# One 256-column matmul in place of two 128-column ones in the state and direct-output products of an S5 layer, with the second partial sum added by VectorE

## The chip, the cores and the metric

The kernel runs on one core of one Trainium2 chip. The metric is the device time of one execution in microseconds (us). Before the change it is 2616.41 us, the median of three runs (2616.41 to 2618.24). In the text TensorE is PE, with PEld for its weight loads, VectorE is DVE, ScalarE is ACT, GpSimd is POOL and SyncE is SP, which issues nearly all DMAs. Each engine works through its own queue strictly in the order in which the program wrote it; engines wait for each other by semaphores.

## The reference

An attention block, a gated linear attention block and an S5 block follow one another on a sequence of 1024 tokens and 1024 channels, in float32. The change lies in the S5 block, whose core is

```
u, z   = split(h @ w_in)                       # 2048 channels each, 128 groups of 16
bu     = u32 . b_bar                           # per group: 16 inputs -> 64 complex states
states = associative_scan(a_l*a_r, a_r*b_l + b_r)
y      = Re(states) . c_re - Im(states) . c_im + d * u32
y      = gelu(y);  y = y * sigmoid(y @ w_glu + b_glu) * silu(z);  out = y @ w_out
```

The kernel computes it in chunks of 8 tokens: 128 chunks, one "step" of the recurrence each. For a group, what a chunk adds to its 128 state numbers (64 real, 64 imaginary) is a product of the chunk's 8 x 16 inputs with a 128x128 matrix W. What a chunk's inputs give directly to its own 8 x 16 outputs is a product with a 128x128 matrix T. What the state at the chunk's start gives to the outputs comes later, from a third matrix V.

## The kernel before

Float32 precision on PE comes from splitting each operand into a rounded high part and a low part: `hi` is a cast by ACT (L179), `lo` the difference by POOL (L187, in some stages DVE). A product then takes three matmuls (`mm3`, L194 to L196): high by high, high by low, low by high, all summed in one place of PSUM.

Groups are worked in octets of 8, so there are 16 octets. The first phase of the S5 block (some 1576 to 1860 us in the trace) is a loop of 19 rounds over `first`. In round i the projection generator `project(i)` makes the inputs u of octet i in two halves of 24 matmuls of 512 columns, evacuates each half by ACT (L2165), and writes them to a DRAM scratch (eight DMAs, L2174). From round 3 on the generator `states(i - 3)` works on the octet three rounds back. The two generators are stepped in turn, so PE sees four stretches in one round, called a pass here:

1. the state product U by W of the octet, 8 groups, 24 matmuls of 128 columns into a PSUM tile `big` of 1024 columns; ACT copies it into the state table X (L2214);
2. the first half of the projection;
3. the direct product U by T, again 24 matmuls of 128 columns; ACT copies it into a staging tile `w` (L2222), and SP writes it to the scratch `syp_d` (L2225);
4. the second half of the projection.

There are two `big` tiles in PSUM, so a product can start when the one two places back has been read out.

U, W, T and the projection's weights come through `WStream`: three raw buffers filled by DMA (`wraw`, L100), a ring of six split pieces (`whl`). `pump(n)` issues further loads and splits up to n pieces in the order of use, as far as the ring has room; `release` makes room. Where the calls to `pump` stand in the program sets where the casts stand in ACT's queue and the subtractions in POOL's. Before, `states` calls `pump(2)` right behind the direct product, ahead of the projection's second half.

Beside this, DVE runs the recurrence over the 128 chunks, for four octets at a time (`scan(k)`, L2238 to L2280). One scan is 29 steps: three empty ones (the first issues a DMA for the table `scL`), 15 turns of five instructions over 256 columns, four steps with seven small turns, which read the table `scLP` in SBUF, and seven fix-up steps. A scan is appended after its fourth octet. `scan_on` puts one step behind each of the first two stretches of a pass and two steps behind each of the other two, so six in a pass, as long as there is a scan to run. From octet 4 on the sixteen passes therefore hold two whole scans and the first eleven turns of the third. In the second phase (z projection and the third product) the same goes on with four steps in a round.

The names that the prediction uses: `pairs`, `add_now` and the new `states` of the changed kernel, `scan_on`, `pump`, and the lines above.

Of the kernel before, what the change touches and what calls it, by code (L numbers as in the profile page):

```python
# [16 lines left out]
OP = mybir.AluOpType  # L17
# [6 lines left out]
P = 128  # L24
# [1352 lines left out]
def pool_of(g, stack, name, bufs=1, side="left"):  # L1377
    return stack.enter_context(g.tc.tile_pool(name=name, bufs=bufs, side=side, reuse_waits="tile"))
# [756 lines left out]
def s5(g, xn3, xstack, out):  # L2135
    nc, A, ws = g.nc, g.A, g.ws
# [5 lines left out]
    u_d, spilled, octet, put_m, put_cols, first = (  # L2142
        q.u_d, q.spilled, q.octet, q.put_m, q.put_cols, q.first)
# [14 lines left out]
    def project(i, ids):  # L2158

        W = ws.take(ids)  # L2160
        stage = stg.tile([P, S], F, name="w4")
        for half in range(2):
            ps = g.bank()
            gemm_tr(g, hT, half, W, 0, P, ps, ids if half else None, True, later)
            nc.scalar.activation(half_of(stage, half, True), ps.rearrange("p (t c) -> p t c", t=8),  # L2165
                                 AF.Copy)
            ws.pump(1)
            if half == 0:
                yield
        if i >= NO:  # L2170
            nc.sync.dma_start(z_d[i - NO], stage)
            return
        for j in range(8):
            nc.sync.dma_start(u_d[:, :, i * 8 + j, :].rearrange("t i c -> i t c"),  # L2174
                              stage[j * 16:j * 16 + 16, :].rearrange("p (t c) -> p t c", t=8))
        spilled[i] = True
# [11 lines left out]
    X = pool_of(g, xp, "s5x").tile([P, P, P], F, name="X")  # L2188
# [15 lines left out]
    for half in range(2):  # L2204
        pglu[half] += [put_cols(w_glu, 16, e * P) for e in range(len(pglu[half]), NO)]
        pout.append([ws.put(1, S, [((slice(None),) * 3, g.kview(w_out, k * P, 1, 0, S))]) for k in range(16)])

    def states(o, ids):

        U, W = ws.take(ids[:2])  # L2210
        ps = g.big().rearrange("p (g n) -> p g n", g=8)
        for j in range(8):
            g.mm3(ps[:, j], [a[:, j, :] for a in W], [a[:, j, :] for a in U], True, True)
        nc.scalar.copy(X[:, 1:P, octet(o)], ps.rearrange("p g n -> p n g")[:, 0:P - 1])  # L2214
        del ps
        yield
        T = ws.take(ids)[2]
        yp = stg.tile([P, S], F, name="w4")
        ps = g.big().rearrange("p (g n) -> p g n", g=8)
        for j in range(8):  # L2220
            g.mm3(ps[:, j], [a[:, j, :] for a in U], [a[:, j, :] for a in T], True, True)
        nc.scalar.copy(yp.rearrange("c (g x) -> c g x", g=8), ps)  # L2222
        del ps
        ws.release(ids)
        nc.sync.dma_start(yp_d[o], yp)  # L2225
        ws.pump(2)

# [57 lines left out]
    def scan_on(n):  # L2285

        while n and scans:
            k, ge = scans[0]
            if next(ge, 0) == 0:
                scans.popleft()  # L2290
                scanned[k] = True
            else:
                n -= 1

    for i, px, pp in first:
        gens = [states(i - LAG, px)] if px else []
        gens.append(project(i, pp) if i else begun)
        for r in range(2):
            for ge in gens:
                next(ge, None)  # L2300
                scan_on(1 + r)
        if px and (i - LAG) % 4 == 3:
            scans.append(((i - LAG) // 4, scan((i - LAG) // 4)))

# [16 lines left out]
    def outputs():  # L2321

        o, ps = sums.popleft()
        Xo = X[:, :, octet(o)]
        gto = lambda a: a.rearrange("p (g t o) -> p g t o", g=8, t=8)
        nc.vector.tensor_tensor(Xo.rearrange("p (g o) t -> p g t o", g=8), gto(parts.pop(o)), gto(ps), OP.add)  # L2326
        del ps
        yield
        nc.scalar.activation(Xo, Xo, AF.Gelu_apprx_tanh)

    ws.hi_eng, ws.lo_eng = ["act"], ["pool"]
    for n, (i, ids) in enumerate(second):
        ge, ou = project(NO + i, ids), outputs() if sums else iter(())
# [16 lines left out]
    yp = ExitStack()  # L2350
# [135 lines left out]
    for half in range(2):  # L2486
        hs = slice(half * 512, half * 512 + 512)
        for e in range(NO):
            k0 = glu_k[0] if half == 0 and e == 0 else 0
            ps = accs.pop(e) if k0 else g.bank()  # L2490
# [25 lines left out]
        for k in range(12):  # L2516
            W = ws.take(pout[half][k:k + 1])[0]
# [10 lines left out]
        W = ws.take(pout[half][12:])  # L2528
# [25 lines left out]
def model_kernel(tc, A):  # L2554
    with ExitStack() as ctx:
        g = G(tc, A, ctx)
        g.x2_d = g.dram.tile([S, D], F, name="x2_d")
        g.x3_d = g.dram.tile([S, D], F, name="x3_d")
        with tc.manual_schedule():
            s5_tables(g)  # L2560
            xs = ExitStack()
            xn2 = block1(g, xs)
            xacc, outs = gla(g, xn2, xs, lambda side: s5_prep(g, side))
            s5(g, xacc, outs, A["out"])
# [40 lines left out]
```

## Time and profile before

| | |
|---|---|
| median of three runs | 2616.41 us |
| the profiled execution: its time, its span | 2615.66 us, 2613.9 us |
| busy in the span: PE, PEld, DVE, ACT, POOL | 92%, 76%, 65%, 42%, 43% |
| granted PE clock, mean over the span | 0.964 |
| first octet's state product starts | 1597.37 us |
| last direct product copied by ACT (L2222) | 1853.82 us |

The span is the stretch from the first to the last instruction of the trace; the execution's own time is 1.8 us more. Busy shares are means over stages with different limits, so the stage of the change is read by itself. A matmul's duration in the trace is its latency; matmuls follow each other faster than that, and what one costs is the distance between starts. "[3.10 <-DVE mm]" behind a row says that the engine stood idle for 3.10 us before it and what ended the wait.

### The profile page before, as it was taken

To read this page: it belongs to the slowest core of one execution; us is meant where nothing else is said; L and a number is where in the kernel's file an instruction comes from. 1 tells how busy PE (TensorE), PEld (TensorE's weight loads), DVE (VectorE), ACT (ScalarE), POOL (GpSimd) and SP (SyncE) were. 2 spreads that over 40 slices of the span, in tenths; PEclk is the share of its full clock that TensorE was granted. 3 is DMA by queue.
4 is the path that set the end of the run, shared out by engine and by line. 5 is a ranking of instruction groups with operands and counts; after the bars stand their busy time and mean duration, and the time that the engine had idled before them with its cause. 6 is when DMAs were issued, how large, how long until landed. Compare 5 with 4: busy or idle time off the path is not lost.

```text
span 2613.9 us, 33041 instructions
## 1 busy us (share of the span) xinstructions
PE 2417.1 (92%) x11817; PEld 1990.4 (76%) x11817; DVE 1708.2 (65%) x3015; ACT 1109.5 (42%) x1812; POOL 1127.5 (43%) x826
## 2 busy tenths in 40 slices
PE   5787977999999999999989899999999899999998
PEld 4665755777777777777777678888888788888887
DVE  5889887777454556785777770389788555425642
ACT  5455683656532122324443443444443533323331
POOL 3517465322211566664444424555554433333431
PEclk8998988999999999999989899999999899999999
DMA  8302124221332645535432316777554644444441
GB/s 263 113 30 62 54 87 154 85 65 56 107 122 84 159 136 152 165 122 177 153 113 85 93 69 164 194 202 201 183 154 146 192 133 121 149 139 146 140 149 57
DMA packets 330173, 338.25 MB, mean 129 GB/s; under 512 B 67366, under 2 KB 248182, under 8 KB 329752
## 3 DMA queue, kind: packets, MB, share of 16 engines
q1 hardware_dynamic: 330008, 336.13, 42.2%
q8 instruction: 93, 1.52, 0.2%
q14 instruction: 72, 0.59, 0.1%
HBM read 239.19 MB, written 96.87 MB: 129 GB/s over the span
## 4 chain that ended last, share of the span: by engine, by line
PE 30%; DVE 10%; issue 5%; DMA 3%; POOL 3%; ACT 2%; SPq 0%; POOLq 0%; DVEq 0%; ACTq 0%
PE mm L194 8%; PE mm L196 8%; PE mm L195 8%; PE big L196 2%; PE big L195 2%; PE big L194 2%; POOL whl L187 2%; DMA w<-syp_d 2%; DVE xacc L1998 1%; DVE X L2326 1%; DVE rs_t L215 1%; DVE mm L2257 1%; POOL rs_h L212 1%; DVE mm L2255 1%; DVE rs_t L216 1%
## 5 line engine op out<-in xcount | busy, mean ns | idle before, releaser
L187 POOL TENSOR_TENSOR whl<-wraw,whl 128x1024 fp32r<-128x1024 f32 x183 | 443.3, 2431 | 606.0 <-ACT whl L179 527.3
L179 ACT CAST whl<-wraw 128x1024 fp32r<-128x1024 f32 (+1 forms) x279 | 288.5, 1048 | 360.9 <-PE mm L196 220.0
L194 PE MATMUL mm<-h_hi,whl 128*128 128x512 f32 x768 | 308.0, 401 | 14.5 <-DVE gT L952 7.8
L196 PE MATMUL mm<-h_hi,whl 128*128 128x512 f32 x768 | 302.0, 393 | 0.0
L195 PE MATMUL mm<-h_lo,whl 128*128 128x512 f32 x768 | 301.4, 392 | 0.0
L194 PE MATMUL mm<-whl,h_hi 128*128 128x512 f32 (+1 forms) x720 | 288.4, 400 | 13.0 <-ACT whl L179 9.6
L195 PE MATMUL mm<-whl,h_hi 128*128 128x512 f32 (+1 forms) x720 | 282.1, 392 | 10.8 <-DVE whl L187 10.8
L196 PE MATMUL mm<-whl,h_lo 128*128 128x512 f32 (+1 forms) x720 | 281.1, 390 | 0.0
L187 DVE TENSOR_TENSOR whl<-wraw,whl 128x1024 fp32r<-128x1024 f32 (+2 forms) x96 | 133.4, 1399 | 147.2 <-ACT whl L179 147.1
L194 PE MATMUL mm<-y_hl,whl 128*128 128x512 f32 x512 | 201.3, 393 | 0.0
L195 PE MATMUL mm<-y_hl,whl 128*128 128x512 f32 x512 | 199.9, 390 | 0.0
L196 PE MATMUL mm<-y_hl,whl 128*128 128x512 f32 x512 | 199.8, 390 | 0.0
L194 PEld LDWEIGHTS mm<-h_hi,whl 128*128 128x128 f32 x768 | 146.0, 190 | 49.5 <-DVE gT L952 8.7
L196 PEld LDWEIGHTS mm<-h_hi,whl 128*128 128x128 f32 x768 | 145.5, 189 | 32.2
L195 PEld LDWEIGHTS mm<-h_lo,whl 128*128 128x128 f32 x768 | 146.1, 190 | 29.4 <-issue 0.5
L194 PEld LDWEIGHTS mm<-whl,h_hi 128*128 128x128 f32 x720 | 137.7, 191 | 40.4 <-ACT whl L179 10.1
L195 PEld LDWEIGHTS mm<-whl,h_hi 128*128 128x128 f32 x720 | 138.0, 192 | 36.9 <-DVE whl L187 12.2
L196 PEld LDWEIGHTS mm<-whl,h_lo 128*128 128x128 f32 x720 | 137.3, 191 | 28.5
L187 POOL TENSOR_TENSOR w<-w 128x512 f32<-128x512 f32 x32 | 55.1, 1722 | 168.2 <-ACT w L2434 168.2
L196 PEld LDWEIGHTS mm<-y_hl,whl 128*128 128x128 f32 x512 | 96.5, 189 | 20.1
L194 PEld LDWEIGHTS mm<-y_hl,whl 128*128 128x128 f32 x512 | 97.0, 189 | 19.4
L195 PEld LDWEIGHTS mm<-y_hl,whl 128*128 128x128 f32 x512 | 96.6, 189 | 19.5
(542 smaller groups left out, 5928.8 us busy)
## 6 DMA issues: line engine op xcount, KB each, us to landing
wraw<-in_s_w_glu_dram SPq DMA_DIRECT2D x64, 512.0 KB, 3.9
wraw<-in_gla_w_in_dram SPq DMA_DIRECT2D x40, 512.0 KB, 4.3
wraw<-in_s_w_in_dram SPq DMA_DIRECT2D x32, 512.0 KB, 5.6
wraw<-in_s_w_out_dram SPq DMA_DIRECT2D x32, 512.0 KB, 3.6
gv_d<-stg SPq DMA_DIRECT2D x32, 256.0 KB, 2.2
v_mat<-vc SPq DMA_DIRECT2D x32, 256.0 KB, 2.6
w_mat<-wo SPq DMA_DIRECT2D x32, 256.0 KB, 2.5
gz_d<-stg SPq DMA_DIRECT2D x32, 256.0 KB, 2.1
```

Source lines behind the costliest of these rows:

```text
L179: nc.scalar.copy(out, in_)
L187: e.tensor_tensor(out, a, b, op)
L194: nc.tensor.matmul(out, lhsT=lhs[0], rhs=rhs[0], start=start, stop=False)
L195: nc.tensor.matmul(out, lhsT=lhs[0], rhs=rhs[1], start=False, stop=False)
L196: nc.tensor.matmul(out, lhsT=lhs[1], rhs=rhs[0], start=False, stop=stop)
L212: nc.gpsimd.tensor_tensor(h, v, self.mhalf[:, :n], OP.pow)
L215: nc.vector.tensor_tensor(t, h, h, OP.mult)
L216: nc.vector.tensor_tensor(t, t, v, OP.mult)
L1998: nc.vector.scalar_tensor_tensor(xs, ps[nh], rst, xs, op0=OP.mult, op1=OP.add)
L2255: nc.vector.tensor_tensor(a, x, wide(L[0], n), OP.mult)
L2257: nc.vector.tensor_tensor(c[half[q]], x[half[1 - q]], wide(L[1][half[1 - q]], n), OP.mult)
L2326: nc.vector.tensor_tensor(Xo.rearrange("p (g o) t -> p g t o", g=8), gto(parts.pop(o)), gto(ps), OP.add)
```

## The change

Both products take `mm2` (in the kernel before, but not used by it) in place of `mm3`. Of a split piece, high and low lie side by side in one tile. For each group `mm2` issues one matmul of 256 columns, which multiplies the high part of the fixed operand by the high and the low part of the moving one, into two neighbouring 128-column places of PSUM; a second matmul of 128 columns adds low by high to the second place. A product so leaves two sums. `pairs` works an octet in two halves of four groups, each half in a `big` tile of its own. ACT copies the first sums to their destination (X or the staging tile), and DVE adds the second sums to that destination in place. These additions are not written at once: they are kept in a list, and `add_now` writes them at the next step of `states`. For the state product that is at the head of the direct product, for the direct product it is in a third step at the end of the round, and with it the DMA to `syp_d` and `pump(2)` move there, behind the projection's second half.

```
+    def add_now():
+        for out, ps in adds:
+            nc.vector.tensor_tensor(out, out, ps, OP.add)
+        adds.clear()
+    def pairs(o, lhs, ids, out):
+        for half in range(2):
+            ps = g.big().rearrange("p (j a n) -> p j a n", j=4, a=2)
+            for j in range(4):
+                k = half * 4 + j
+                g.mm2(ps[:, j], [a[:, k, :] for a in lhs], ws.pairs[ids][:, :, k, :])
+            for i in range(2):
+                dst, src = out(half, ps[:, :, i])
+                if i:
+                    adds.append((dst, src))
+                else:
+                    nc.scalar.copy(dst, src)
...
     def states(o, ids):
         U, W = ws.take(ids[:2])
-        ps = g.big().rearrange("p (g n) -> p g n", g=8)
-        for j in range(8):
-            g.mm3(ps[:, j], [a[:, j, :] for a in W], [a[:, j, :] for a in U], True, True)
-        nc.scalar.copy(X[:, 1:P, octet(o)], ps.rearrange("p g n -> p n g")[:, 0:P - 1])
...
+        add_now()
+        pairs(o, W, ids[0], lambda half, ps: (X[:, 1:P, o * 8 + half * 4:o * 8 + half * 4 + 4],
+                                              ps.rearrange("p g n -> p n g")[:, 0:P - 1]))
+        yield
+        ws.take(ids)
         yp = stg.tile([P, S], F, name="w4")
-        ps = g.big().rearrange("p (g n) -> p g n", g=8)
-        for j in range(8):
-            g.mm3(ps[:, j], [a[:, j, :] for a in U], [a[:, j, :] for a in T], True, True)
-        nc.scalar.copy(yp.rearrange("c (g x) -> c g x", g=8), ps)
...
+        add_now()
+        pairs(o, U, ids[2], lambda half, ps: (yp[:, half * 512:half * 512 + 512].rearrange("c (g x) -> c g x", g=4), ps))
         ws.release(ids)
+        yield
+        add_now()
         nc.sync.dma_start(yp_d[o], yp)
         ws.pump(2)
...
+        for ge in gens:
+            next(ge, None)
```

The last two lines stand at the end of a round in the loop over `first`; they run the third step.

The instructions move on two engines. On DVE, at the end of octet 6, where the first scan's turns end and its small turns begin, the queue before is the scan alone:

```order
L2255 TENSOR_TENSOR mm<-X,mm 128x256
L2257 TENSOR_TENSOR mm<-X,mm 64x256 x2
L2258 TENSOR_TENSOR X<-X,mm 128x8x32
L2259 TENSOR_TENSOR X<-X,mm 128x8x32
L2255 TENSOR_TENSOR mm<-X,scLP 128x32
L2257 TENSOR_TENSOR mm<-X,scLP 64x32 x2
L2258 TENSOR_TENSOR X<-X,mm 128x32
L2259 TENSOR_TENSOR X<-X,mm 128x32
```

At the same place of the changed kernel (its scan's lines are 20 higher) the additions of octet 6's direct product (`w`, from the two `big` tiles) stand between the turns:

```order
L2275 TENSOR_TENSOR mm<-X,mm 128x256
L2277 TENSOR_TENSOR mm<-X,mm 64x256 x2
L2278 TENSOR_TENSOR X<-X,mm 128x8x32
L2279 TENSOR_TENSOR X<-X,mm 128x8x32
L2213 TENSOR_TENSOR w_14906<-w_14906,big_14909 128x512
L2213 TENSOR_TENSOR w_14906<-w_14906,big_14919 128x512
L2275 TENSOR_TENSOR mm<-X,scLP 128x32
L2277 TENSOR_TENSOR mm<-X,scLP 64x32 x2
L2278 TENSOR_TENSOR X<-X,mm 128x32
L2279 TENSOR_TENSOR X<-X,mm 128x32
```

Two additions of a product, which no scan step needs, now stand in the scan's queue; four of them come in a pass. On ACT, in the pass of octet 1, the queue before is as follows; `whl_14219` is the weight piece of the next round's projection, and the second L2165 is the evacuation of this round's second half:

```order
L2214 COPY X_13785<-big1024_14133 128x127x8
L2165 ACTIVATE w4_14159<-mm_14160 128x8x64
L2222 COPY w4_14188<-big1024_14189 128x1024
L179 CAST whl_14216<-wraw_14107 128x1024
L179 CAST whl_14219<-wraw_14120 128x1024
L179 CAST whl_14258<-wraw_14186 128x1024
L2165 ACTIVATE w4_14159<-mm_14222 128x8x64
L179 CAST whl_14264<-wraw_14247 128x1024
```

In the changed kernel the same pass reads as follows, and the weight piece of the next projection is `whl_14228`:

```order
L2229 COPY X_13785<-big1024_14123 128x127x4
L2229 COPY X_13785<-big1024_14133 128x127x4
L2165 ACTIVATE w4_14143<-mm_14144 128x8x64
L2229 COPY w4_14174<-big1024_14177 128x512
L2229 COPY w4_14174<-big1024_14187 128x512
L179 CAST whl_14222<-wraw_14108 128x1024
L2165 ACTIVATE w4_14143<-mm_14197 128x8x64
L179 CAST whl_14228<-wraw_14170 128x1024
L179 CAST whl_14251<-wraw_14172 128x1024
L179 CAST whl_14254<-wraw_14226 128x1024
```

The cast of the next projection's weights has moved from ahead of the second half's evacuation to behind it. POOL's subtractions follow the casts in the same order.

## Rows read from the trace of the kernel before

**Rows 1.** Windows: stretch, length, busy and count of each engine, clock, DMA share, GB/s.

```profile
1600.00:1620.00 20.00, 20.00 (x114) 17.37 (x114) 0.00 (x0) 9.51 (x12) 11.89 (x5) 1.00 0.78 200
1680.00:1700.00 20.00, 20.00 (x122) 17.69 (x122) 18.52 (x44) 9.44 (x11) 12.53 (x6) 1.00 0.75 209
```

**Rows 2.** Timeline of PE, octet 0: start, duration, engine, line, operation, wait before.

```profile
1597.37 0.22 PE L194 MATMUL big<-whl 128*128 128x128 f32 x1
...
1599.88 0.28 PE L196 MATMUL big<-whl 128*128 128x128 f32 x1
1600.00 0.45 PE L194 MATMUL mm<-h_hi,whl 128*128 128x512 f32 x1
...
1605.55 0.22 PE L194 MATMUL big<-whl 128*128 128x128 f32 x1
```

**Rows 3.** Timeline of PE, 256-column matmuls of the attention.

```profile
474.30 0.28 PE L1234 MATMUL mm<-pth,v_hl 128*128 128x256 f32 x1
...
474.54 0.28 PE L1234 MATMUL mm<-pth,v_hl 128*128 128x256 f32 x1
```

**Rows 4.** Timeline of DVE, the first scan and the start of the second.

```profile
1675.92 0.23 DVE L2249 COPY mm<-scL 128x64 f32<-128x64 f32 x1 [104.11 <-ACT whl L179]
...
1678.58 0.43 DVE L2255 TENSOR_TENSOR mm<-X,mm 128x256 f32<-128x256 f32 x1
...
1710.80 0.28 DVE L2255 TENSOR_TENSOR mm<-X,scLP 128x32 f32<-128x32 f32 x1
1711.12 2.54 DVE L2257 TENSOR_TENSOR mm<-X,scLP 64x32 f32<-64x32 f32 x2
...
1717.65 0.43 DVE L2257 TENSOR_TENSOR mm<-X,scLP 64x32 f32<-64x32 f32 x2
...
1725.26 0.20 DVE L2273 COPY mm<-X 128x32 f32<-128x32 f32 x1
...
1726.84 0.65 DVE L2280 TENSOR_TENSOR X<-X,mm 128x480 f32<-128x480 f32 x1
1727.53 0.20 DVE L2278 TENSOR_TENSOR mm<-scL,mm 128x32 f32<-128x32 f32 x1
...
1728.99 0.18 DVE L2273 COPY mm<-X 128x32 f32<-128x32 f32 x1
...
1756.88 0.23 DVE L2249 COPY mm<-scL 128x64 f32<-128x64 f32 x1 [5.50 <-DMA scL<-scan_d]
```

**Rows 5.** Groups by form on DVE: shapes, count, busy us, mean ns, idle before.

```profile
L2326 DVE TENSOR_TENSOR X<-w,big 128x1024 f32<-128x1024 f32 x16 | 32.0, 1998 | 17.8 <-DMA w<-syp_d 17.8
...
L298 DVE SCALAR_TENSOR_TENSOR h_lo<-mm,cols,h_hi 128x512 fp32r<-128x512 f32 x32 | 23.2, 748 | 8.2 <-ACT h_hi L297 7.7
...
L952 DVE SCALAR_TENSOR_TENSOR gT<-mm,cols,gT 128x512 f32<-128x512 f32 x8 | 5.7, 743 | 2.1 <-PE mm L951 2.0
```

**Rows 6.** Groups by form, 1600 to 1860 us, on POOL and ACT.

```profile
L187 POOL TENSOR_TENSOR whl<-wraw,whl 128x1024 fp32r<-128x1024 f32 x63 | 149.9, 2396 | 103.5 <-ACT whl L179 93.6 <-DMA wraw<-in_s_w_in_dram 5.7 <-DMA su_d<-w 4.1
...
L179 ACT CAST whl<-wraw 128x1024 fp32r<-128x1024 f32 x64 | 65.5, 1050 | 79.9 <-DMA wraw<-su_d 47.3 <-DMA wraw<-w_mat 23.6 <-POOL whl L187 7.0
...
L2165 ACT ACTIVATE w<-mm 128x512 f32<-128x512 f32 x33 | 19.6, 594 | 37.4 <-issue 33.5 <-PE mm L196 3.8
```

**Rows 7.** Timeline of SP: DMA issues of octets 3 to 5.

```profile
1664.30 3.64 SPq L100 DMA_DIRECT2D wraw<-kp_d  x8
...
1668.54 4.19 SPq L2174 DMA_DIRECT2D su_d<-w  x8
1672.83 0.57 SPq L2238 DMA_DIRECT2D scL<-scan_d  x1
...
1676.21 0.42 SPq L2225 DMA_DIRECT2D syp_d<-w  x1
```

**Rows 8.** Timeline of PE after a wait, end of the second phase.

```profile
2031.27 0.50 PE L194 MATMUL mm<-h_hi,whl 128*128 128x512 f32 x1 [3.10 <-DVE mm L2279]
...
2035.25 0.40 PE L195 MATMUL mm<-h_lo,whl 128*128 128x512 f32 x1
```

More of the change, by code (lines that the diff above doesn't have):

```diff
@@ L2206, in s5 @@
         pout.append([ws.put(1, S, [((slice(None),) * 3, g.kview(w_out, k * P, 1, 0, S))]) for k in range(16)])
+    adds = []
+    def add_now():
[14 more added lines that the diff above has]
+                    nc.scalar.copy(dst, src)
     def states(o, ids):
         U, W = ws.take(ids[:2])
-        ps = g.big().rearrange("p (g n) -> p g n", g=8)
-        for j in range(8):
-            g.mm3(ps[:, j], [a[:, j, :] for a in W], [a[:, j, :] for a in U], True, True)
-        nc.scalar.copy(X[:, 1:P, octet(o)], ps.rearrange("p g n -> p n g")[:, 0:P - 1])
-        del ps
+        add_now()
+        pairs(o, W, ids[0], lambda half, ps: (X[:, 1:P, o * 8 + half * 4:o * 8 + half * 4 + 4],
+                                              ps.rearrange("p g n -> p n g")[:, 0:P - 1]))
         yield
-        T = ws.take(ids)[2]
+        ws.take(ids)
         yp = stg.tile([P, S], F, name="w4")
-        ps = g.big().rearrange("p (g n) -> p g n", g=8)
-        for j in range(8):
-            g.mm3(ps[:, j], [a[:, j, :] for a in U], [a[:, j, :] for a in T], True, True)
-        nc.scalar.copy(yp.rearrange("c (g x) -> c g x", g=8), ps)
-        del ps
+        add_now()
+        pairs(o, U, ids[2], lambda half, ps: (yp[:, half * 512:half * 512 + 512].rearrange("c (g x) -> c g x", g=4), ps))
         ws.release(ids)
+        yield
+        add_now()
         nc.sync.dma_start(yp_d[o], yp)
```

## The prediction

> **What bounds the kernel now.** I read the busy shares first, then the windows of the stage, then the timelines of PE, DVE and SP in it. The page gives PE 92% of the span, but the stage decides. In the windows [rows 1] the reader is to see that PE is busy 20.00 of 20 us at a clock of 1.00, both in the first octets, where DVE does nothing, and during a scan, where DVE is busy 18.52 of 20. So PE bounds the first phase and never waits, and DVE has almost as much to do. Before, nothing ties the two: a scan writes X, which nobody reads before the second phase, and ACT frees the `big` tiles. In PE's timeline [rows 2] a product of 24 matmuls of 128 columns takes 2.63 us (1597.37 to 1600.00), a projection half of 24 with 512 columns 5.55 us. A pass is 2 x 2.63 + 2 x 5.55 = 16.36 us.
>
> **What PE gains.** A 128-column matmul costs 2.63 / 24 = 0.11 us. Matmuls of 256 columns follow each other in 0.12 us (two in 474.30 to 474.54) [rows 3]. A product of eight pairs then takes 8 x (0.12 + 0.11) = 1.84 us, 0.79 less; 32 products give 25 us, and a pass would be 14.78 us.
>
> **What DVE is given.** Four additions a pass. No row has one, so I bound it. The last scan steps add 480 columns of PSUM to X in 0.69 us from start to start (1726.84 to 1727.53) [rows 4]; scaled to 512 that is 0.73. The other bound is L2326, which writes X one element at a time, 512 bytes apart, in 1998 ns for 1024 [rows 5], so 0.99 for 508; it would apply to the two additions into X. I take 0.73 for all, since runs of four lie nearer to the scan's runs of 32: 2.92 us a pass.
>
> [...] By the dearer reading the sum would be 6 us higher (0.26 us x 2 in 11 passes).
>
> **What ties PE to DVE.** A `big` half is now free only when DVE has added it, and both halves of each product take the two tiles. So each product waits for the additions of the product before, and these stand in DVE's queue behind the scan steps: two steps ahead of the state product's, four ahead of the direct product's. A pass of six turns costs DVE, with the turn at 2.30 us (1678.58 to 1710.80 are 14 turns), 13.8 + 2.9 = 16.7 us. The small turns take 14.5 us in four steps (1710.80 to 1725.26), a fix-up step 3.73 us (1725.26 to 1728.99) [rows 4]. A pass of fix-up steps comes to over 20 us. With 14.78 us on PE, DVE is the bound wherever a scan runs.
>
> **What moves on ACT and POOL.** The next projection's weights are cast behind the second half's evacuation. From that half's end: evacuation 0.59, cast 1.05, subtraction 2.40 us [rows 6], so the low part is ready after 4.04 us. PE reaches the projection after 1.84 us and needs the low part at its third matmul, 0.46 later; it waits 1.7 us, and a pass that DVE doesn't hold takes 16.5 us instead of 14.78. Where DVE holds the state product back by more than 1.7, this costs nothing. The ring's other pieces have most of a pass to come in.
>
> **SP.** The `syp_d` DMA now waits for DVE, and T's eight loads stand behind it. The scan's table `scL` for the first scan comes after them: from the end of octet 3's pass 0.59 (evacuation), 4.19 (`su_d`), 0.42 (`syp_d`), 3.64 (T), 3.09 from its issue to the copy that reads it [rows 4, 7], together 11.9 us. Now additions stand behind that copy in DVE's queue, and PE waits for them.
>
> **The sum, along DVE's queue.** Octets 0 to 3 have no scan: 14.8 + 3 x 16.5 = 64.3 against 65.4 us: -1.1. Octets 4 to 8: 11.9 until the table is there, then one scan, 75.5 us (1675.92 to 1725.26, and seven fix-up steps), and 18 additions among it, 13.1: 100.5 against 5 x 16.36 = 81.8: +18.7. Octets 9 to 13: state product 1.84, last copy 0.59, two additions 1.46, the second scan 75.5 and 18 additions 13.1: 92.5 against 81.8: +10.7. Octets 14 and 15, counted from DVE's last addition for octet 13: the third table lands 7.9 us after PE ends that pass (0.59 + 4.19 + 3.09), some 2.4 of which are over by then: 5.5; copy and one turn 2.66 (1675.92 to 1678.58), two additions, four turns 9.2, and one addition that frees a tile: 19.6; octet 15's own pass 14.8: 34.4 against 32.7: +1.7. Together +30.0.
>
> One item I shorten. In the small turns some instructions whose operands both lie in SBUF took 2.1 us too long (two in 2.54 us at 1711.12, in 0.43 at 1717.65) [rows 4], three such in the first scan, 6.3 us. The excess has nearly the length of a POOL subtraction (2.40) [rows 6]. POOL has as many of these in a pass as before while passes grow longer, so I take a third off: -4.2 for both scans. Forecast: +25.8 us.
>
> The second phase I cost at nothing. There DVE waits 17.8 us for DMAs ahead of L2326 [rows 5], so a scan that comes a few us earlier or later is evened out; if that cover is gone, it is 5 us either way.
>
> The profiled execution took 2615.66 us, 1.8 more than its span and 0.8 less than the median, so the sum is added to the median: 2616.4 + 25.8 = 2642 us.
>
> **The likeliest case's own range.** Below: the small turns without any excess (-8.4), and the first table in time, so that its turns start behind the state product's additions at 3.9 us (-8): +9. Above: dearer X additions (+6), the excess as before (+4), and PE's clock. After a wait of 3.10 us PE ran at the lower of its two levels: ten matmuls took 3.98 us (2031.27 to 2035.25) where ten at 0.23 take 2.3 [rows 8]. Five waits of over 3 us are in my sum (octets 4, 7, 8, 12, 14), so up to +8. That makes +44, and 2625 to 2660.
>
> **Rivals.** (1) Faster: the additions find room and PE keeps its gain, 25 us: 2591. The point from which it decides is DVE's queue in a pass: at or under 14.8 us PE never waits. For it speaks that DVE is idle in octets 0 to 3 and in gaps of 5.5 us between scans (1756.88) [rows 4]; against it that six turns alone are 13.8 and fix-up steps more. It would need half a pass of buffering, and there are only two tiles. 8%. (2) A wash: no excess, tables in time, and the cast chain hidden in the three early passes too (-5): +4, 2620. For it: each part is a wait that a shift of queues can remove. Against: it needs all three. 12%. (3) The clock: PE comes out of every long wait at the lower level and the delay reaches DVE's additions, with X additions at the dear bound: 2660. Against: where DVE binds, PE has slack. 12%. (4) The change doesn't do what it says: a 256-column matmul with two sums costs as two of 128 (0.22), so that a product stays at 2.6 us: about six passes that PE bounds lose 1.6 us each, +10, 2652. Against it stand the 0.12 us of [rows 3]. 4%. The forecast keeps 64%.
>
> **The numbers.** A measurement of this kernel tells 0.2%, 5 us, from no change. Faster: rival 1 and a little of 2, 10%. Within: most of 2, 8%. Slower: 82%. The range 2616 to 2662 leaves out rival 1, a third of 2 and half of 3, 18%.
>
> **What the profile will show.** PE: 256-column matmuls at 0.12 us, products at 1.84 us; a wait of about 1.7 us at the third matmul of the first projection half in octets 1 to 4, ended by POOL; from octet 5 on waits at the `big` matmuls ended by DVE's additions, longest (8 us or more) in octets 8 and 13, at the fix-up steps. DVE: additions near 0.7 us, no idle time within a scan. The first phase should last about 288 us in place of 262 and the rest stay. If PE's waits for DVE sum to under 15 us, or if additions into X take 1 us, the mechanism or its size is wrong.

## The result and the profile after

| | changed | before |
|---|---|---|
| median (lowest to highest) | 2645.93 us (2644.14 to 2651.06), 4 runs | 2617.32 us (2616.41 to 2621.31), 4 runs |
| ratio, 95% interval | 1.0108, 1.0096 to 1.0120 | |
| span of the profiled execution, granted PE clock | 2643.3 us, 0.954 | 2613.9 us, 0.964 |
| first state product to the end of octet 15's pass | 1596.17 to 1888.1: 291.9 us | 1597.37 to 1859.1: 261.8 us |

The change made the kernel 28.6 us slower. All of it lies in the first phase, which is 30.1 us longer. Behind it nothing moved: PE's last wait of the second phase [rows 8] comes at the same place, as long as before, 29.0 us later:

```profile
2060.26 0.50 PE L194 MATMUL mm<-h_hi,whl 128*128 128x512 f32 x1 [3.11 <-DVE mm L2299]
```

PE got what the change offers it. In its timeline (start, duration, engine, line, operation) octet 0's state product, to be held against [rows 2], reads:

```profile
1596.17 0.28 PE L201 MATMUL big<-whl 128*128 128x256 f32 x1
1596.29 0.22 PE L202 MATMUL big<-whl 128*128 128x128 f32 x1
1596.35 0.34 PE L201 MATMUL big<-whl 128*128 128x256 f32 x1
...
1597.97 0.45 PE L194 MATMUL mm<-h_hi,whl 128*128 128x512 f32 x1
```

The product takes 1.80 us in place of 2.63, a pair of matmuls 0.23. A pass without a wait is 2 x 1.80 + 2 x 5.53 = 14.65 us; octet 0's pass takes 14.72. But the windows of the stage (columns as in [rows 1]; the first two stretches are those shown there) show PE no longer full:

```profile
1600.00:1620.00 20.00, 18.30 (x97) 15.28 (x96) 3.93 (x6) 10.03 (x15) 13.46 (x6) 1.00 0.73 188
1680.00:1700.00 20.00, 17.96 (x95) 15.87 (x96) 18.80 (x42) 8.06 (x12) 9.47 (x4) 0.91 0.63 172
1736.00:1761.00 25.00, 19.71 (x90) 17.21 (x91) 21.96 (x53) 8.45 (x12) 12.28 (x6) 0.79 0.61 145
1832.00:1857.00 25.00, 19.52 (x98) 17.04 (x98) 21.78 (x53) 7.69 (x11) 9.77 (x5) 0.80 0.54 134
```

PE is busy 92%, 90%, 79% and 78% of these stretches, and the clock, 1.00 before, falls to 0.79. The list of waits between 1576 and 1900 us (who waited for whom: us in all, times, longest) names two releasers of PE (a third wait, for additions into X, is 0.5 us):

```profile
PE big L201 <- DVE w L2213: 18.6, 5, 7.2
PE mm L196 <- POOL whl L187: 17.7, 11, 1.7
```

Two kinds of place, one for each. In octet 1 PE comes to the third matmul of the first projection half and waits for the low part of the weights; at the start of octet 8's state product, and longest at that of octet 13's, it waits for VectorE's additions of the direct product before, which hold the `big` tile:

```profile
1613.00 0.40 PE L195 MATMUL mm<-h_lo,whl 128*128 128x512 f32 x1
1615.10 0.50 PE L196 MATMUL mm<-h_hi,whl 128*128 128x512 f32 x1 [1.70 <-POOL whl L187]
1615.43 0.40 PE L194 MATMUL mm<-h_hi,whl 128*128 128x512 f32 x1
...
1737.95 0.55 PE L201 MATMUL big<-whl 128*128 128x256 f32 x1 [4.49 <-DVE w L2213]
1738.30 0.31 PE L202 MATMUL big<-whl 128*128 128x128 f32 x1
1738.41 0.52 PE L201 MATMUL big<-whl 128*128 128x256 f32 x1
1738.73 0.31 PE L202 MATMUL big<-whl 128*128 128x128 f32 x1
1738.83 0.52 PE L201 MATMUL big<-whl 128*128 128x256 f32 x1
...
1837.48 0.55 PE L201 MATMUL big<-whl 128*128 128x256 f32 x1 [7.21 <-DVE w L2213]
```

Behind the wait of 4.49 us a pair takes 0.42 us (1738.41 to 1738.83) where it took 0.23: PE has come out of the wait at the lower of its two levels. In the whole phase 36 matmuls of 512 columns follow each other in 0.43 instead of 0.23 us and four products take 3.07 to 3.45 us instead of 1.80. With the shorter delays where the level changes, the lower level costs some 10 us in the projection halves and 6 in the products, 16 in all.

VectorE's timeline shows the cause of the second kind. The first scan starts at 1674.05 and has no gap until its end; the additions stand between its steps:

```profile
1674.05 0.23 DVE L2269 COPY mm<-scL 128x64 f32<-128x64 f32 x1 [6.22 <-DMA scL<-scan_d]
...
1681.20 1.28 DVE L2213 TENSOR_TENSOR w<-w,big 128x512 f32<-128x512 f32 x2
...
1697.46 1.28 DVE L2213 TENSOR_TENSOR w<-w,big 128x512 f32<-128x512 f32 x2
...
1737.12 1.28 DVE L2213 TENSOR_TENSOR w<-w,big 128x512 f32<-128x512 f32 x2
1738.32 0.19 DVE L2293 COPY mm<-X 128x32 f32<-128x32 f32 x1
...
1757.52 0.65 DVE L2300 TENSOR_TENSOR X<-X,mm 128x480 f32<-128x480 f32 x1
```

The reader is to see two things. Between the two rows of 1681.20 and 1697.46 lie the additions of one pass and six turns, 16.26 us: VectorE alone makes a turn's pass as long as PE's 16.36 of before. And the additions of 1737.12 end the wait of PE at 1737.95.

### The profile page after: what moved, and what is told of

Its sections match the earlier page's. It is cut to its first block, busy times and chain, and to the rows that moved or that the text cites. A ratio compares the mean times of both kernels' runs of the same rounds, so it can differ in the third digit from the quotient of the medians.

```text
span 2643.3 us, 32722 instructions
## 1 busy us (share of the span) xinstructions
PE 2412.2 (91%) x11561; PEld 1976.1 (75%) x11561; DVE 1753.8 (66%) x3079; ACT 1113.0 (42%) x1844; POOL 1125.7 (43%) x826
## 4 chain that ended last, share of the span: by engine, by line
PE 47%; DVE 24%; issue 9%; ACT 7%; DMA 6%; POOL 5%; SPq 2%; POOLq 0%; DVEq 0%; ACTq 0%
PE mm L196 12%; PE mm L194 12%; PE mm L195 12%; POOL whl L187 2%; DMA w<-syp_d 2%; ACT tku L830 1%; PE big L196 1%; PE big L194 1%; PE big L195 1%; DVE mm L2277 1%; PE mm L1684 1%; ACT whl L179 1%; PE big L1169 1%; DVE xacc L1998 1%; DVE mm L2275 1%
## 5 line engine op out<-in xcount | busy, mean ns | idle before, releaser
L194 PE MATMUL mm<-h_hi,whl 128*128 128x512 f32 x768 | 311.4, 405 | 13.6 <-DVE gT L952 7.0
L196 PE MATMUL mm<-h_hi,whl 128*128 128x512 f32 x768 | 306.2, 399 | 17.7 <-POOL whl L187 17.7
L195 PEld LDWEIGHTS mm<-whl,h_hi 128*128 128x128 f32 x720 | 138.7, 193 | 36.8 <-DVE whl L187 11.7
L196 PEld LDWEIGHTS mm<-y_hl,whl 128*128 128x128 f32 x512 | 96.5, 189 | 20.1
```

The lines of the kernel that those rows point to most:

```text
L194: nc.tensor.matmul(out, lhsT=lhs[0], rhs=rhs[0], start=start, stop=False)
L195: nc.tensor.matmul(out, lhsT=lhs[0], rhs=rhs[1], start=False, stop=False)
L196: nc.tensor.matmul(out, lhsT=lhs[1], rhs=rhs[0], start=False, stop=stop)
```

## The experiments

A run is compared with runs of the kernel before on the same chip, whose medians were 2620.84 (e runs), 2619.73 (g runs) and 2619.66 us (h runs). The theories of the first four runs: A, VectorE's queue holds the `big` tiles and besides the weights are cast late, because they are asked for (`pump(2)`) a stretch later; B, the moved `pump` is the whole loss; C, VectorE is; D, the additions cost PE even where VectorE is idle.

**e1: the weights asked for where they were.**

```
         ws.release(ids)
+        ws.pump(2)
         yield
         add_now()
         nc.sync.dma_start(yp_d[o], yp)
-        ws.pump(2)
```

> The changed kernel with the one call of pump(2) put back behind the direct product, ahead of the projection's second half. The additions stay where they are. Theory A (two mechanisms: DVE's queue holds the big tiles, and the late cast of the next projection's weights lengthens a pass by 1.7 us or more): the eleven waits of 1.7 us of PE for POOL go, passes of octets 0 to 3 come down to 14.6 us, passes with fix-up steps stay at 19 to 25 us; the first phase loses 9 to 19 us against the kernel before, time 2626 to 2636. Rival B (the moved pump is the whole loss): the first phase takes 234 us, time about 2590. Rival C (DVE alone, the POOL waits only fill time in which PE would wait for DVE): no change from the changed kernel, 2642 to 2648.

Measured 2661.40 us, ratio 1.0166 (1.0147 to 1.0185): slower than the change as made. Every theory missed it. In the list of waits (1576 to 1900 us) PE waits for additions 31.3 us in 10, where the change has 19.1 in 6, and VectorE waits for the scan's table `scL`:

```profile
PE big L201 <- DVE w L2213: 18.5, 6, 5.8
PE big L201 <- DVE X L2213: 12.8, 4, 6.6
DVE mm L2269 <- DMA scL<-scan_d: 23.3, 3, 10.6
```

In the change the last of these reads:

```profile
DVE mm L2269 <- DMA scL<-scan_d: 9.7, 2, 6.2
```

VectorE so stands 13.6 us longer for the tables, and the additions behind them in its queue hold PE. On SP the first table's DMA now stands behind T's loads and behind the spills:

```profile
1669.44 3.63 SPq L100 DMA_DIRECT2D wraw<-kp_d  x8
...
1673.68 4.18 SPq L2174 DMA_DIRECT2D su_d<-w  x8
...
1678.42 0.57 SPq L2258 DMA_DIRECT2D scL<-scan_d  x1
```

It is issued 14.2 us after the end of octet 3's pass; in the change it was 9.5. Octets 0 to 3 take 66.3 us in both, octets 4 to 8 102.5 (the change: 96.5), 9 to 13 97.1 (95.8), 14 and 15 39.4 (33.4). This is read from the two traces; no run tests it.

**e2: the change without its additions.** The loop in `add_now` is taken out; X and the direct output lack the second sums.

```
     def add_now():
-        for out, ps in adds:
-            nc.vector.tensor_tensor(out, out, ps, OP.add)
         adds.clear()
```

> The changed kernel without the additions by DVE: the second sums are computed on PE and left unread, so the products lack their low terms. The pump stays where the change put it. Theory A: PE never waits for DVE in the first phase, all passes from octet 1 on take 16.6 us, a little more where the clock falls after a wait of 1.7 us; 1 to 13 us slower than before, 2618 to 2630. Rival B (pump alone): as the changed kernel, 2642 to 2648. Rival C (DVE alone): about 2590.

Measured 2627.85 us, ratio 1.0032 (1.0020 to 1.0043). This lies in A's range. Without any addition, then, the change still loses 7 us. PE's waits, and two places of its timeline, octets 2 and 3:

```profile
PE mm L196 <- POOL whl L187: 25.6, 15, 1.7
```

```profile
1635.41 0.50 PE L196 MATMUL mm<-h_hi,whl 128*128 128x512 f32 x1 [1.70 <-POOL whl L187]
...
1652.07 0.75 PE L196 MATMUL mm<-h_hi,whl 128*128 128x512 f32 x1 [1.71 <-POOL whl L187]
1652.62 0.63 PE L194 MATMUL mm<-h_hi,whl 128*128 128x512 f32 x1
1653.05 0.63 PE L195 MATMUL mm<-h_lo,whl 128*128 128x512 f32 x1
```

Every pass but the first has the wait of 1.7 us for the weights' low part and is 16.7 us long; in octets 3, 7, 11 and 15 the matmuls behind the same wait stand 0.43 us apart, and the pass is 18.3. So the late weights alone take back the whole gain, once no addition is there to hide them.

**e3: both, no additions and the weights asked for early** (the edits of e1 and e2 together).

> Both: no additions by DVE (the second sums are left unread, as in the run without additions) and the pump put back. Theory A: PE waits for nobody in the first phase; 16 passes of 14.6 us, 27 us less than before, 2589. If a wait is left that neither theory names, it is over 2595, and the trace shows it. If the 256-column matmul costs more than 0.12 us beside other work, products are longer than 1.8 us.

Measured 2633.98 us, ratio 1.0053 (1.0032 to 1.0074): not the 2589 that A forecast. PE still waited for POOL's low parts, 27.2 us in 13 waits. The list of waits has a row that the kernel before has at 8.1 us in 4 waits only, ACT's copy of the direct product into its staging tile:

```profile
ACT w L2227 <- DMA su_d<-w: 54.9, 13, 6.1
```

Its timeline, in one pass, with the rows of SP (its DMA issues), ACT, POOL and PE that make the chain:

```profile
1633.78 3.63 SPq L100 DMA_DIRECT2D wraw<-kp_d  x8
1637.51 0.40 SPq L100 DMA_DIRECT2D wraw<-in_s_w_in_dram  x1
1638.01 5.13 SPq L2174 DMA_DIRECT2D su_d<-w  x8
...
1645.16 1.07 ACT L2227 COPY w<-big 128x512 f32<-128x512 f32 x2 [4.12 <-DMA su_d<-w]
1646.12 2.01 ACT L179 CAST whl<-wraw 128x1024 fp32r<-128x1024 f32 x2
...
1647.26 9.57 POOL L187 TENSOR_TENSOR whl<-wraw,whl 128x1024 fp32r<-128x1024 f32 x4 [8.61 <-ACT whl L179]
...
1652.02 0.50 PE L196 MATMUL mm<-h_hi,whl 128*128 128x512 f32 x1 [1.98 <-POOL whl L187]
```

The three `w4` tiles go round: a direct product's copy writes the tile that the projection's output of the round before has left, which is free when its eight spills have landed. The spills stand on SP behind nine loads, and at PE's faster pace PE finishes the direct product first. The copy stops ACT, the casts stand behind the copy, POOL behind the casts, PE behind POOL.

**e4: the change in octets 0 to 3 only**, where VectorE has nothing else to do, weights asked for early, octets 4 to 15 as before.

> The changed products in octets 0 to 3 alone, in which no scan runs, with the pump ahead of the second half; octets 4 to 15 as in the kernel before. Theory A: nothing waits, four passes take 14.6 us in place of 16.36, 7 us less than before: 2609 to 2611. Rival D (the additions cost PE time even where DVE is idle, by their wait for ACT's copies): same as before within 2 us.

Measured 2623.26 us, ratio 1.0013 (1.0003 to 1.0022): no gain where one was due. The passes were 15.3, 15.3, 20.7 and 15.5 us, and octet 4's still 20.0; ACT's copies waited for the spills as in e3 (13.0 us in 3 waits), PE for POOL, up to 2.8 us. D's number nearly came (2.4 us over the kernel before), but not its mechanism: PE waited 0.4 us for an addition.

Hence theory T: with early weights it is the staging tile that delays them. Rival S: the supply itself, loads and casts, can give no more than a pass in some 16.7 us. The next four runs give the direct product a tile of its own ("w4c"), the projection's outputs take turns with the other two:

```
-        yp = stg.tile([P, S], F, name="w4")
+        yp = w4([P, S], "c")
```

**g3: the kernel before with that tile, the control.**

> The kernel before with nothing but the direct product's own staging tile. Both theories: passes at the matmuls' 16.36 us as before, where the copy waited 8 us in four waits for the spills without TensorE waiting: 2615-2619 us. A time outside it would say that the tile's new order costs or gives something by itself, and the other runs of this call would have to be read against it.

Measured 2635.32 us, ratio 1.0066 (1.0053 to 1.0078), outside both. My edit had also fixed which tile the GLU stage takes for what, and PE waits there for tiles that it did not wait for before:

```profile
PE mm L194 <- ACT w4c L2507: 7.4, 1, 7.4
PE mm L194 <- ACT w4a L2507: 4.6, 1, 4.6
```

These 12 us and a longer octet 1 (19.5 us) are the control's cost, so the three runs of this tile are read against 2635.32.

**g1: as e3, with its own tile, and `syp_d` sent straight behind the product.**

> Leaves out the additions of the second sums (so X and the direct output lack the part with the other moving half). Weights are asked for right behind the direct product and its output is sent right there, as in the kernel before; and the direct product's staging tile is no longer one of a rotation of three with the projection's, but always the same one, so that its ScalarE copy waits for the tile's own send of the pass before and no longer for the eight spills of the pass before. Theory T (in the two runs with the weights asked for early the ScalarE copy stood waiting for those spills, 55 us in 13 waits, with the weight casts behind it, so that the weights came late): with its own tile the passes come down to 14.6 to 15.0 us, the first phase to 235-241 us against 262 of before, and the time to 2591-2597 us. Rival S (the supply itself, loads on the queue and casts, can give no more than one pass in some 16.7 us whatever tile the copy takes): as the run with early weights without additions, 2625-2636 us.

Measured 2621.65 us, ratio 1.0014 (1.0005 to 1.0023); against the control -13.7. The time lies outside both ranges; the passes, 14.6 to 14.8 us in half of the octets, are those of T, and S says that there can be none.

**g2: as e4, with its own tile and the additions straight behind the copies.**

> The kernel before with the 256-column matmuls in octets 0 to 3 only, where VectorE has no scan to do, the additions put out straight behind the ScalarE copies, and the direct product's staging tile its own. Theory T: four passes at 14.7 to 15.0 instead of 16.36 us, 5.5 to 6.7 us less: 2610-2613 us. Rival S: the weights are late as in the run of the first four octets alone, no gain: 2618-2624 us.

Measured 2633.20 us, ratio 1.0054 (1.0042 to 1.0067): 2.1 under the control, too little to judge by.

**g4: the whole change with its own tile, weights early, the direct product's additions and its send between the projection's halves.**

> The whole change with additions, weights asked for right behind the direct product as before, the direct product's own staging tile, and its additions and send put out between the two halves of the projection, ahead of the spills on the queue. Theory T: what is left is VectorE's queue: octets 0 to 3 at 14.7 to 15, the octets with a scan as slow as the changed kernel's or a little better, first phase 275-285 us: 2630-2640 us, and TensorE's waits are for VectorE's additions. Rival S: 2655-2665 us, like the changed kernel with early weights.

Measured 2672.04 us, ratio 1.0203 (1.0187 to 1.0218), 36.7 over the control and over both ranges. The weights came in time, against S: PE's waits are now for VectorE alone, bar one of 2.8 us. Two of them are for the direct product's additions, 7.2 us. The rest, and VectorE's own waits for the scan's tables:

```profile
PE big L201 <- DVE X L2220: 36.6, 12, 7.7
DVE mm L2276 <- DMA scL<-scan_d: 22.0, 3, 13.2
```

So the additions eat the gain without any late weights too. From octet 4 on they stand behind scan steps in VectorE's queue, and behind its waits for tables, which are 22.0 us here as against 9.7 in the change; how the loss divides between the two was not told apart.

The last three runs mend the control: one of the three tiles is kept by the direct product through the first phase only.

```
+        if not held:
+            held.append(stg.tile([P, S], F, name="w4"))
+        yp = held[0]
...
+    held.clear()
     parts, sums = {}, deque()
```

**h1: the kernel before with the kept tile.**

> The kernel before with one staging tile of the three kept by the direct product through all sixteen octets; the other two go on by turns, and all three do again in the later stages (the control of the call before, which had 15 us of its own, changed the order of the tiles in those stages too). Both theories: 2615-2621 us, no pass changed. If it costs 10 us or more again, the kept tile itself costs that and not the later stages.

Measured 2618.78 us, ratio 0.9998 (0.9988 to 1.0008): the control is neutral, and each pass is 16.4 us.

**h3: no additions, weights early, kept tile.**

> Leaves out the additions of the second sums (X and the direct output lack the part with the other moving half). All sixteen octets with 256-column matmuls, weights asked for early, the direct product's kept tile. Theory T: passes at 14.6 to 15 us with three or four longer ones where the h_lo operations of the next half and the scan's table come (16 to 18), first phase 240-246 us: 2596-2604 us, the first run of the set under the kernel before. Rival S: 2617 us or more.

Measured 2604.96 us, ratio 0.9944 (0.9926 to 0.9963), 1 us above T's range. PE's waits for POOL are gone; the copy's wait for the spills is 0.3 us in place of 54.9. What is left stands one step earlier in the chain, in ACT and PE:

```profile
ACT whl L179 <- DMA wraw<-su_d: 85.2, 16, 7.5
PE big L201 <- ACT X L2227: 9.0, 8, 2.6
ACT w L2227 <- DMA su_d<-w: 0.3, 1, 0.3
```

ACT's cast of the U piece waits for its load from `su_d`, and the copy of the state product stands behind that cast. Passes are 14.6 us at best, but octets 7 and 11 take 20.5 and 18.5: PE waits there for the copy of the state product, 2.6 and 2.0 us, and goes on at the lower level, with pairs 0.43 us apart. Why these two copies are the latest was not followed further.

**h2: octets 0 to 3 only, kept tile, additions straight behind the copies.**

> As the control of this call, with the 256-column matmuls in octets 0 to 3 only and their additions put out straight behind the ScalarE copies. Theory T (the spills behind the loads held the direct product's copy; VectorE idle in these octets): four passes at 14.7 to 15.2 instead of 16.36 us: 5 to 6.7 us under the control, 2610-2614 us. Rival S (the supply of weights): 2618-2624 us.

Measured 2615.57 us, ratio 0.9984 (0.9974 to 0.9995), between the two forecasts. It is the one version that leaves nothing out and is under the kernel before, by 4 us; under its control by 3.2. Passes 14.8, 18.3, 14.6, 14.6, together 3.1 us less than four of 16.36. Octet 1 keeps the rest; in the timeline of DVE and PE:

```profile
1620.01 1.28 DVE L2213 TENSOR_TENSOR X<-X,big 128x508 f32<-128x508 f32 x2 [12.61 <-ACT X L2229]
...
1620.75 0.39 PE L201 MATMUL big<-whl 128*128 128x256 f32 x1 [1.83 <-DVE X L2213]
```

VectorE is idle there and waits for ACT's copy, which stands behind the casts. After three more pairs PE falls to the lower level: the product takes 2.82 us, the projection half behind it 6.16 instead of 5.53.

## Why the prediction was right

The forecast was 2642 us, the measurement is 2645.93, slower by the mechanism named. Point by point:

- **PE's gain.** 1.80 us a product in place of the forecast 1.84, so a 256-column matmul did not cost as two of 128 (rival 4 falls). Rival 1 would have needed passes at that pace with the additions in; with them in all octets the phase was 291.9 us (the change), 305.3 (e1) or 300.5 (g4). 16 passes of 14.65 are 234.4, 27 us less than before; the phase took 291.9, so 57.5 us came back, 36.8 of them waits of PE and some 16 the lower clock.
- **The additions.** The groups of 1596 to 1890 us (busy us, mean ns) have them at 684 and 678 ns:

```profile
L2213 DVE TENSOR_TENSOR w<-w,big 128x512 f32<-128x512 f32 x32 | 20.9, 684 | 17.1 <-ACT w L2229 14.0 <-DMA wraw<-kp_d 2.9 <-DMA wraw<-in_s_w_in_dram 0.2
...
L2213 DVE TENSOR_TENSOR X<-X,big 128x508 f32<-128x508 f32 x32 | 20.5, 678 | 74.8 <-ACT X L2229 74.7
```

  Two behind each other take 1.20 us (1737.12 to 1738.32), 0.60 each where I took 0.73. Those into X (678 ns) cost no more than those into rows (684), though they read single floats 1 KB apart from PSUM: the dear bound of 0.99 falls.
- **A pass of six turns**: 16.26 us on VectorE, 16.7 forecast. **The first table**: 11.6 us after octet 4's start (1662.42 to 1674.05), 11.9 forecast. **The cast chain**: a wait of 1.70 us, 1.7 forecast.
- **The blocks.** Octets 0 to 3: 66.3 (forecast 64.3), 4 to 8: 96.5 (100.5), 9 to 13: 95.8 (92.5), 14 and 15: 33.4 (34.4), together 292.0 against 291.7. That the sum comes so near is in part luck, since what was too dear and what was too cheap cancel. The first scan took 84.05 us (1674.05 to 1758.10) for 88.6: its additions were cheaper, and two small instructions were too long, where the sum has three. The second had four, these two among them, where others take 0.43 together:

```profile
1816.89 4.68 DVE L2277 TENSOR_TENSOR mm<-X,scLP 64x32 f32<-64x32 f32 x2
```

  Both scans together have some 12 us of this, as much as the sum had at first (12.6). The third that I took off (4.2 us) was taken off wrongly, and is about what the forecast lacks: 25.8 for 28.6.
- **Where a step was wrong.** I had the weights' wait in octets 1 to 4 only, "where DVE holds the state product back by more than 1.7, this costs nothing". In a pass of turns VectorE's 16.26 and the cast chain's 16.6 us are as good as equal, so neither hides the other, and the wait stands in octets 6, 7, 10, 11, 12 and 14 as well, with 0.7 us of it in octet 15. PE waits for additions of 0.5 us and more in octets 5, 8, 9, 12, 13 and 15 only. The longest wait for the additions was 7.2 us, not 8 or more.
- **The clock** was an upper bound only, up to +8. The trace has 16 us at the lower level, also behind waits of 1.7 us, which I had not counted. The terms that were too dear (additions, the first scan) made up for it.
- **What the runs add.** The sum put 29.4 of its 30.0 us into VectorE's queue (octets 4 to 13). Taking the additions out (e2) gives back 21.6 of the 28.6 us, but nothing of the gain: with late weights the kernel is still 7.0 us over the kernel before. With the weights in time as well (h3) it is 14.7 under it, another 21.7 us. With weights in time and additions (g4 against its control) the loss is 36.7, more than the change's own 28.6, though there the additions stand at another place of the queue and wait longer for the tables. So the late weights eat the gain by themselves (e2), and so do the additions with what they wait for in VectorE's queue (g4). In the change the two costs partly cover each other: where an octet starts with a wait of 2.8 us or more for additions (5, 8, 9 and 13), the weights are not waited for.
- **What failed** is my theory A on e1: I took the later `pump` for a pure loss. It also keeps the loads behind the spills on SP, and so the staging tile free in time. In e1 the copy waits for the spills (29.8 us in 7; the change has no such wait), and VectorE 13.6 us longer for the scan's tables; its phase is 13.4 us longer than the change's. That is the size of what it loses beyond the change, 12.0 us (40.6 against 28.6, each over the kernel before on its own chip).

## What to carry to other kernels

When an engine that never waits is made 10% faster, look for every loop that ran just under its old pace: here VectorE's turns with the additions (16.3 us), the cast chain behind the moved request (16.6) and the round trip of a staging tile through the DMA queue (17.3 on the mean of e3's passes) all came to about the old pass of 16.36, and each one had to go before 14.65 could be had. Taking one away shows the next, and can look like a loss (e1, e3); a run without the disputed work (e2) and a neutral control (h1) tell them apart. Here the faster product paid only where the engine that it burdens is idle: four octets of sixteen, 4 us.

## What the runs showed of the hardware

- The granted clock after one and the same wait is not always the same. In e2 the wait of 1.70 to 1.72 us comes 15 times, at the same matmul; 11 times the matmuls behind it follow at 0.23 us and four times at 0.43, 1.6 us a time; the windows around two of these waits have a clock of 1.00 (1634 to 1638 us) and 0.57 (1652 to 1656).
- A VectorE addition from PSUM costs 0.68 us by its own row and 0.60 from start to start when another stands behind it. The strides of those into X (runs of four floats 512 bytes apart in SBUF, single floats 1 KB apart in PSUM) did not show: 678 ns for 508 elements, and 684 for 512 of the others.
